# Ten 32-byte tiles made ahead of the weights' pool: 320 bytes further on for three pools

## The chip, the cores and the metric

The kernel runs on one core of one Trainium2 chip. The metric is device time of one execution in microseconds; the kernel before takes 1852.08 us (median of 3 runs, 1851.85 to 1852.86). The engines named below are PE (TensorE: matmuls, and beside them PEld, its weight loads), ACT (ScalarE), DVE (VectorE), POOL (GpSimd) and SP (SyncE, which here issues most DMAs). On-chip memory (SBUF) has 128 partitions; a tile lies at the same byte address in each of them, and "address" below is that byte address in a partition.

## What is computed

One layer on x of 256 rows by 2048 columns, in float32:

```python
x = x + 0.5 * swiglu(rms_norm(x, ffn1_norm), ffn1_w_gate, ffn1_w_up, ffn1_w_down)
proj = rms_norm(x, mix_norm) @ w_in                      # u | q | k | v, 1024 columns each
y_ssm = s5_mixer(u, ...)                                 # diagonal state space, gelu, GLU
y_sb = stick_breaking_attention(rms_norm(q), rms_norm(k), v)     # 8 heads of 128
x = x + concat(rms_norm(y_ssm), rms_norm(y_sb)) @ w_out
x = x + 0.5 * swiglu(rms_norm(x, ffn2_norm), ffn2_w_gate, ffn2_w_up, ffn2_w_down)
gate = sigmoid(rms_norm(x, ple_norm) @ w_ple_gate)
x = x + rms_norm((p @ w_ple_proj) * gate, ple_post_norm)
```

The two feed-forward blocks have an inner width of 5632; their six weight matrices are most of the work.

## The kernel before, in words

**Products in two parts.** Each float32 operand is split into a high part in the matmul's own format (fp32r) and a low part, the rest: `split` (line 178) casts on ACT at line 181 (`whi` from `raw`) and subtracts on DVE at line 184 (`wlo`). A product is then three matmuls: high by high (line 305), high by low (306), low by high (310). In every one of them the weights (`whi`, `wlo`; 512 columns) are the moving operand and the activations (`nhi`, `nlo`, `hhi`, `hlo`; 128 by 128) the stationary one, which a weight load brings in just before. Only the GLU of the state-space branch (lines 1369 to 1378) has it the other way round, with 256 moving columns.

**Where weights go.** SP loads 1 MB of weights at a time into one of five `raw` buffers; ACT and DVE make `whi` and `wlo` of it, two rows of 512 at a time, in four buffers each; `gemm_half` (line 298) runs 12 matmuls on each such pair for both halves of the rows of x, or 6 for one half.

**`Seven`.** In the feed-forward blocks, two neighbouring blocks of columns are worked together (class `Seven`, line 446). Its `column` (524) is `gemm_half` for one half of the rows at a time. Its `chunk` (490) takes two 1 MB loads and does with seven products of six matmuls (lines 480, 481, 483 in `product`) what would be eight: four of the seven have sums of weights as moving operand. DVE makes a sum (`sum`, line 487), ACT casts it into `shi`, DVE subtracts into `slo`. The stationary operand of a chunk is a plain activation or a sum of activations; both lie in the tiles of the activations.

**The last stage.** `w_ple_proj` is multiplied by `p`, split into two tiles `pT`. For the last block of columns `gemm_resident` (line 341) keeps half of the gate's weights and all of the projection's in tiles `whi`, `wlo` of the stage's own memory.

**Where tiles lie.** Pools take their memory one behind the other in the order in which they are made (lines 52 to 56). Memory of single stages (`phase`, line 73: sums of the feed-forward blocks, their `hT`, the state-space and attention tiles, the last stage) begins behind the last of them. A tile's size is rounded up to 32 bytes, and the program keeps 1152 bytes for itself at the start. So in the kernel before:

| pool | tiles | begins at | begins modulo 512 |
|---|---|---|---|
| const | six masks of 512 bytes, then 1416 (rounded to 1440) and 128 | 1152 | 128 |
| wts | 5 `raw` or `x` of 8192; 4 `whi` and 4 `wlo` of 4096 | 5792 | 160 |
| act | 4 `nhi`, 4 `nlo`, 2 `hhi`, 2 `hlo`, 4096 each | 79520 | 160 |
| com | `h` twice and `sg` of 4096, `sq` of 2048, `mid` of 8192 | 128672 | 160 |
| small | 10 `sm` of 32 | 151200 | 160 |
| stages | `shi`, `slo`, `sum`, `hT`, `pT`, `q`, `k`, ... | 151520 | 480 |

Tiles of wts, act, com and most of the stages are multiples of 512 bytes, and so are the steps inside them that the matmuls take (512, 1024 or 2048 bytes): every such operand begins where its pool begins, modulo 512.

**What sets the order.** The order of each engine's instructions follows the program text; small pieces of work are put between the matmuls by counted steps (`put_off`, `step`). Engines wait for each other by semaphores.

Of the kernel before, what the change touches and what calls it, by code (L numbers as in the profile page):

```python
# [33 lines left out]
def layer_kernel(ctx: ExitStack, tc: tile.TileContext, a: dict, shapes: dict, out: bass.AP):  # L34
# [15 lines left out]
    assert TT == 2 and NP == 64 and HC == 16 and DH == P and NC == 64 and SW == NH * DH  # L50

    cpool = ctx.enter_context(tc.tile_pool(name="const", bufs=1))
    wp = ctx.enter_context(tc.tile_pool(name="wts", bufs=4))
    actp = ctx.enter_context(tc.tile_pool(name="act", bufs=1))
    comp = ctx.enter_context(tc.tile_pool(name="com", bufs=1))
    smp = ctx.enter_context(tc.tile_pool(name="small", bufs=10))
    dramp = ctx.enter_context(tc.tile_pool(name="scratch", bufs=1, space=bass.MemoryType.DRAM))
    accp = ctx.enter_context(tc.tile_pool(name="acc", bufs=4, space=bass.MemoryType.PSUM))
    auxp = ctx.enter_context(tc.tile_pool(name="aux", bufs=2, space=bass.MemoryType.PSUM))
# [1602 lines left out]
```

## Time and profile before

| | |
|---|---|
| median of the runs | 1852.08 us (1851.85 to 1852.86) |
| the profiled execution's own time | 1852.7 us |
| its span, first to last instruction | 1850.6 us |
| PE busy | 1838.3 us, 99% of the span, 9032 matmuls |
| DVE busy | 1460.6 us, 79% |
| ACT busy | 1027.4 us, 56% |
| DMA | 406.36 MB, mean 220 GB/s |

The profile's page has the span in total and in slices, the chain of work that ended last, and groups of instructions by line and tile. [...] What a matmul costs when PE never stops is the step from its start to the start of the next one, which the timeline shows: start in us, length in us, engine, line, operation, tiles, count. A row with x2 or x4 holds that many matmuls in a row.

### The profile page before, as it was taken

What the parts mean: (1) busy time and instruction counts of PE and PEld (TensorE: products, weight loads), DVE (VectorE), ACT (ScalarE), POOL (GpSimd) and SP (SyncE); (2) the same over time, 40 slices, a digit from 0 to 9 for tenths busy, and PEclk for the clock granted to TensorE, in tenths of its full rate; (3) what the DMA queues carried; (4) which work ended last, traced back from release to release, by engine and by line L of the source; (5) the groups of instructions that cost most, each with busy time, mean ns of one, the idle gap of its engine ahead of it and who ended that gap; (6) DMA issues with size and microseconds to landing.
All of it is one profiled execution on the core that took longest, in us unless ns stands there. A gap on an engine that the chain in (4) does not pass through costs nothing.

```text
span 1850.6 us, 23946 instructions
## 1 busy us (share of the span) xinstructions
PE 1838.3 (99%) x9032; PEld 1518.5 (82%) x9032; DVE 1460.6 (79%) x1718; ACT 1027.4 (56%) x1187; POOL 63.3 (3%) x108
## 2 busy tenths in 40 slices
PE   9999999999999999999999999999999999999998
PEld 7888888778888888888897888888888888888887
DVE  8967665998888876687567798989898978887665
ACT  7444443655564656365685565655555555565654
POOL 0011000000000000010021000000000000000000
PEclk9999999999999999999999999999999999999999
DMA  9888868566756567675646776665656675666663
GB/s 334 281 274 277 252 217 246 173 228 200 241 196 213 192 217 248 190 262 166 216 142 218 224 262 216 235 206 198 218 198 219 207 244 185 223 195 217 208 219 125
DMA packets 232307, 406.36 MB, mean 220 GB/s; under 512 B 26784, under 2 KB 50720, under 8 KB 231904
## 3 DMA queue, kind: packets, MB, share of 16 engines
q1 hardware_dynamic: 227824, 392.81, 63.8%
q0 software_dynamic: 3648, 10.62, 1.8%
q8 instruction: 70, 1.15, 0.2%
q10 hardware_dynamic: 720, 1.41, 0.2%
q14 instruction: 45, 0.37, 0.1%
HBM read 373.46 MB, written 11.93 MB: 208 GB/s over the span
## 4 chain that ended last, share of the span: by engine, by line
PE 92%; DVE 3%; DMA 2%; ACT 2%; SPq 1%; issue 1%; DVEq 0%; ACTq 0%
PE acc L305 18%; PE acc L310 18%; PE acc L306 18%; PE aux L305 7%; PE aux L306 7%; PE aux L310 7%; PE acc L480 3%; PE acc L481 2%; PE acc L483 2%; PE aux L480 2%; PE aux L483 2%; PE aux L481 2%; DVE wlo L184 1%; SPq L1170 1%; DMA raw<-in_w_in 1%
## 5 line engine op out<-in xcount | busy, mean ns | idle before, releaser
L181 ACT CAST whi<-raw 128x1024 fp32r<-128x1024 f32 x639 | 668.1, 1052 | 684.8 <-PE acc L306 388.9
L184 DVE TENSOR_TENSOR wlo<-raw,whi 128x1024 fp32r<-128x1024 f32 x639 | 772.0, 1221 | 297.9 <-ACT whi L181 295.1
L305 PE MATMUL acc<-whi,nhi 128*128 128x512 f32 x1232 | 482.9, 392 | 1.8 <-ACT whi L181 1.7
L306 PE MATMUL acc<-whi,nlo 128*128 128x512 f32 x1232 | 479.9, 390 | 0.0
L310 PE MATMUL acc<-wlo,nhi 128*128 128x512 f32 x1232 | 340.6, 389 | 0.2 <-DVE wlo L184 0.2
L305 PEld LDWEIGHTS acc<-whi,nhi 128*128 128x128 f32 x1232 | 231.5, 188 | 52.2 <-ACT whi L181 3.0
L310 PEld LDWEIGHTS acc<-wlo,nhi 128*128 128x128 f32 x1232 | 231.2, 188 | 48.8 <-DVE wlo L184 0.6
L306 PEld LDWEIGHTS acc<-whi,nlo 128*128 128x128 f32 x1232 | 231.6, 188 | 47.2
L306 PE MATMUL acc<-whi,hlo 128*128 128x512 f32 x376 | 146.4, 389 | 0.0
L305 PE MATMUL acc<-whi,hhi 128*128 128x512 f32 x376 | 146.3, 389 | 0.0
L181 ACT CAST shi<-sum 128x1024 fp32r<-128x1024 f32 x108 | 113.4, 1052 | 43.1 <-DVE sum L487 39.6
L306 PE MATMUL aux<-whi,hlo 128*128 128x512 f32 x344 | 133.8, 389 | 0.0
L305 PE MATMUL aux<-whi,hhi 128*128 128x512 f32 x344 | 133.8, 389 | 0.0
L184 DVE TENSOR_TENSOR slo<-sum,shi 128x1024 fp32r<-128x1024 f32 x108 | 130.9, 1216 | 0.6 <-ACT shi L181 0.5
L310 PE MATMUL acc<-wlo,hhi 128*128 128x512 f32 x376 | 114.6, 389 | 0.2 <-DVE wlo L184 0.2
L310 PE MATMUL aux<-wlo,hhi 128*128 128x512 f32 x344 | 106.0, 389 | 0.0
L306 PE MATMUL aux<-whi,nlo 128*128 128x512 f32 x240 | 93.4, 389 | 0.0
L305 PE MATMUL aux<-whi,nhi 128*128 128x512 f32 x240 | 93.4, 389 | 0.0
L306 PEld LDWEIGHTS acc<-whi,hlo 128*128 128x128 f32 x376 | 70.6, 188 | 15.1 <-DVE hlo L184 0.4
L310 PEld LDWEIGHTS acc<-wlo,hhi 128*128 128x128 f32 x376 | 70.5, 188 | 15.2 <-DVE wlo L184 0.6
L305 PEld LDWEIGHTS acc<-whi,hhi 128*128 128x128 f32 x376 | 70.6, 188 | 14.6
L306 PEld LDWEIGHTS aux<-whi,hlo 128*128 128x128 f32 x344 | 64.6, 188 | 13.5
(345 smaller groups left out, 2162.6 us busy)
## 6 DMA issues: line engine op xcount, KB each, us to landing
raw<-in_ffn_w_up SPq DMA_DIRECT2D x88, 1024.0 KB, 5.8
raw<-in_ffn_w_down SPq DMA_DIRECT2D x88, 1024.0 KB, 5.1
raw<-in_ffn_w_gate SPq DMA_DIRECT2D x86, 1024.0 KB, 6.2
raw<-in_w_in SPq DMA_DIRECT2D x32, 1024.0 KB, 5.7
raw<-in_w_out SPq DMA_DIRECT2D x16, 1024.0 KB, 5.3
raw<-in_w_ple_gate SPq DMA_DIRECT2D x16, 1024.0 KB, 5.1
hT<-mid SPq DMA_DIRECT2D x160, 64.0 KB, 3.5
h<-mid SPq DMA_DIRECT2D x176, 32.0 KB, 3.6
```

What stands on the lines that cost most here:

```text
L181: copy = nc.scalar.copy(hi, src)
L184: nc.vector.tensor_tensor(out=lo, in0=src, in1=hi.bitcast(F32), op=ALU.subtract)
L305: nc.tensor.matmul(ps[t], lhsT=lh, rhs=hi[:, j, cols], start=start and j == 0, stop=False)
L306: nc.tensor.matmul(ps[t], lhsT=ll, rhs=hi[:, j, cols], start=False, stop=False)
L310: nc.tensor.matmul(ps[t], lhsT=lh, rhs=lo[:, j, cols], start=False, stop=stop and j == 1)
L480: nc.tensor.matmul(ps, lhsT=lh[j], rhs=hi[:, j], start=begin and j == 0, stop=False)
L481: nc.tensor.matmul(ps, lhsT=ll[j], rhs=hi[:, j], start=False, stop=False)
L483: nc.tensor.matmul(ps, lhsT=lh[j], rhs=lo[:, j], start=False, stop=z in final and j == 1)
L1170: nc.sync.dma_start(zt[0][p1 : p1 + HC, z], sv[p0 : p0 + HC, r % 2 * 2 + r // 2])
```

## The change

The pool `small` is made directly behind `const`, ahead of `wts`, instead of behind `com`. Its ten tiles of 32 bytes now lie at 5792, and wts, act and com begin 320 bytes further on, at 6112, 79840 and 128992, which is 480 modulo 512. The stages begin where they did, at 151520, also 480 modulo 512. `const` stays at 128. No instruction, size, buffer count or wait is written differently.

```diff
     cpool = ctx.enter_context(tc.tile_pool(name="const", bufs=1))
+    smp = ctx.enter_context(tc.tile_pool(name="small", bufs=10))
     wp = ctx.enter_context(tc.tile_pool(name="wts", bufs=4))
     actp = ctx.enter_context(tc.tile_pool(name="act", bufs=1))
     comp = ctx.enter_context(tc.tile_pool(name="com", bufs=1))
-    smp = ctx.enter_context(tc.tile_pool(name="small", bufs=10))
```

## The prediction

> **What bounds the kernel now.** First the page's totals and its chain of waits, then the list of who waited for whom.
>
> ```profile
> span 1850.6 us, 23946 instructions
> PE 1838.3 (99%) x9032; PEld 1518.5 (82%) x9032; DVE 1460.6 (79%) x1718; ACT 1027.4 (56%) x1187; POOL 63.3 (3%) x108
> PEclk9999999999999999999999999999999999999999
> PE 92%; DVE 3%; DMA 2%; ACT 2%; SPq 1%; issue 1%; DVEq 0%; ACTq 0%
> ```
> ```profile
> ACT whi L181 <- PE acc L306: 388.9, 272, 3.0
> ACT whi L181 <- DMA raw<-in_w_in: 13.0, 4, 8.5
> PEld acc L480 <- ACT shi L181: 3.5, 2, 2.1
> PEld aux L480 <- ACT shi L181: 1.9, 3, 1.3
> PEld aux L483 <- DVE slo L184: 0.6, 1, 0.6
> ```
>
> PE is busy in 99% of the span, with the granted clock in its top tenth in every slice, and is 92% of the chain. ACT waits 388.9 us for PE to free a `whi` buffer; PE waits for its makers in a handful of places only. So the time is the number of matmuls times their step, and I look for what sets the step. In the timeline of PE, four stretches without a wait, with operands that begin at different places (the table of pools gives the places):
>
> ```profile
> 1150.11 0.39 PE L305 MATMUL acc<-whi,nhi 128*128 128x512 f32 x1
> 1150.33 0.39 PE L306 MATMUL acc<-whi,nlo 128*128 128x512 f32 x1
> 1150.56 0.39 PE L305 MATMUL acc<-whi,nhi 128*128 128x512 f32 x1
> 1150.79 0.39 PE L306 MATMUL acc<-whi,nlo 128*128 128x512 f32 x1
> 1151.01 0.62 PE L310 MATMUL acc<-wlo,nhi 128*128 128x512 f32 x2
> 1151.47 0.39 PE L305 MATMUL acc<-whi,nhi 128*128 128x512 f32 x1
> ...
> 1163.71 0.39 PE L305 MATMUL aux<-whi,nhi 128*128 128x512 f32 x1
> ```
> ```profile
> 1785.90 0.40 PE L305 MATMUL acc<-whi,pT 128*128 128x512 f32 x1
> ...
> 1788.70 0.40 PE L305 MATMUL acc<-whi,pT 128*128 128x512 f32 x1
> ...
> 1791.50 0.39 PE L305 MATMUL acc<-whi,nhi 128*128 128x512 f32 x1
> ...
> 1813.29 0.40 PE L305 MATMUL acc<-whi,pT 128*128 128x512 f32 x1
> ...
> 1816.09 0.40 PE L305 MATMUL acc<-whi,nhi 128*128 128x512 f32 x1
> ...
> 1821.60 0.39 PE L305 MATMUL acc<-whi,nhi 128*128 128x512 f32 x1
> ```
>
> - Both operands at 160 modulo 512 (weights in wts, activations in act): ten groups of six from 1150.11 to 1163.71, 13.60 us / 60 = **226.7 ns** a matmul.
> - Moving at 160, stationary at 480 (`pT`, from 1785.90): two blocks of 12 in 5.60 us, **233.3 ns**. The block from 1813.29 to 1816.09 says the same: 2.80 / 12.
> - Moving at 480, stationary at 160 (the resident `whi` and `wlo` of the last stage, 24 of them from 1816.09 to 1821.60): 5.51 / 24 = **229.6 ns**.
>
> Width, type and clock are the same in all three; what differs is where the operands begin. Unlike operands cost 2.9 to 6.6 ns a matmul. What both at 480 would cost, which is what the change makes, is seen only with 256 columns, in the last stage; beside it the GLU, both at 160:
>
> ```profile
> 923.82 0.28 PE L1369 MATMUL acc<-hhi,whi 128*128 128x256 f32 x1
> ...
> 925.50 1.12 PE L1378 MATMUL acc<-hhi,wlo 128*128 128x256 f32 x8
> ```
> ```profile
> 1840.10 0.28 PE L305 MATMUL acc<-whi,pT 128*128 128x256 f32 x1
> ...
> 1840.58 0.40 PE L310 MATMUL acc<-wlo,pT 128*128 128x256 f32 x2
> 1840.82 1.02 PE L1554 MATMUL aux<-x,ident 128*128 128x512 f32 x2
> ```
>
> Both at 160: 14 matmuls in 1.68 us, 120.0 ns. Both at 480: 6 in 0.72 us, 120.0 ns. So what counts in these rows is whether the two begin alike, not where.
>
> **The change, part by part.** It adds and removes no instruction, DMA, buffer or wait, and moves none past another on a queue; it moves wts, act and com by 320 bytes, and the ten small tiles ahead of them.
>
> *Products with operands in wts and act.* These are nearly all; they are alike before (160) and after (480). I take 0 for them, by the two equal rows of 120.0 ns; the other bound stands in the last rival.
>
> *Chunks of `Seven`.* The sums lie in the stages (480), their partners in act (160): unlike now, alike after. One chunk without a wait, from its first product with a sum:
>
> ```profile
> 1091.27 0.40 PE L480 MATMUL acc<-shi,nhi 128*128 128x512 f32 x1
> ...
> 1096.78 0.40 PE L480 MATMUL acc<-whi,hhi 128*128 128x512 f32 x1
> ...
> 1099.55 0.39 PE L305 MATMUL acc<-whi,nhi 128*128 128x512 f32 x1
> ```
> ```profile
> L181 ACT CAST whi<-raw 128x1024 fp32r<-128x1024 f32 x639 | 668.1, 1052 | 684.8 <-PE acc L306 388.9 <-PE aux L306 146.0 <-PE acc L481 61.3
> L181 ACT CAST shi<-sum 128x1024 fp32r<-128x1024 f32 x108 | 113.4, 1052 | 43.1 <-DVE sum L487 39.6 <-PE acc L481 2.7 <-issue 0.3
> L181 ACT CAST hhi<-hT 128x1024 fp32r<-128x1024 f32 x56 | 58.4, 1043 | 0.9 <-PE aux L310 0.8
> ```
>
> The four products with sums (24 matmuls) take 5.51 us, 229.6 ns each, like the resident weights. The two behind them have both operands at 160 and still take 2.77 us / 12 = 231 ns: a disturbed sequence needs a dozen matmuls to fall back to 226.7. Together 36 in 8.28 us, where 36 x 226.7 = 8.16: **0.12 us a chunk**. There are 108 casts of sums, four a chunk, so 27 chunks: 3.24 us. Rounding of the rows (0.01 us) leaves 3.0 to 3.5.
>
> *The last stage.* `pT` in three blocks, 36 x 6.6 ns = 0.24 us; resident weights against activations, 24 for each half of the rows, 48 x 2.9 ns = 0.14 us; the falling back behind them, by half a chunk's tail, 0.07 us. Together 0.45 us.
>
> *The casts and subtractions.* `whi` from `raw` (both at 160) and `shi` from `sum` (both at 480) take 1052 ns alike; `hhi` from `hT`, unlike today, 1043. When it becomes alike I allow 9 ns more for 56 of them, 0.5 us of ACT, hidden: ACT is at 56% and waits for PE. If that cover were gone it would be 0.5 us.
>
> *DMAs into moved tiles.*
>
> ```profile
> raw<-in_ffn_w_up SPq DMA_DIRECT2D x88, 1024.0 KB, 5.8
> hT<-mid SPq DMA_DIRECT2D x32, 32.0 KB, 3.9
> h<-mid SPq DMA_DIRECT2D x176, 32.0 KB, 3.6
> ```
>
> Between tiles that begin unlike (`mid` to `hT`) 32 KB land in 3.9 us, between like ones (`mid` to `h`) in 3.6. The change would make the former like the latter; 0.3 us nobody waits for, since `hT` is read in the later half of a feed-forward block. The weights' DMAs keep their sizes; that 320 bytes change a 5.8 us transfer shows in no row, so from both sides I use that same 0.3 us. ACT's four waits for `w_in` (13.0 us) are the place where it would be felt: 4 x 0.3 = 1.2 us either way; I take 0.
>
> *The masks* stay at 128 and were unlike their partners before (160 or 480); they stay unlike. 0.
>
> Sum: 3.24 + 0.45 = **3.7 us less**. The profiled execution's own time is 1852.7 us (2.1 us more than its span) and would become 1849.0; it lies 0.6 us above the median, so the median becomes 1852.1 - 3.7 = **1848.4 us**.
>
> [...]
>
> **The rivals.** The measurement of this kernel can tell about 0.2% from no change, 3.7 us: a faster result is one below 1848.4, which is just where the sum ends.
>
> *The gain is kept whole* (0.56): 3.4 to 4.2 us with the rounding and 0.2 us from settling behind other short waits. 1847.9 to 1848.7.
>
> *Part of it becomes waiting* (0.26). In a chunk the sums come just in time from DVE and ACT. The rows of PEld show six such waits. There, an earlier PE waits longer: up to 0.12 us each, 0.7 us in all; as much again if chunks that now just don't wait begin to. 1848.7 to 1849.9. Against it: with six waits, at least 21 of 27 chunks have none.
>
> *Nothing changes* (0.10). The extra steps would belong to sums and to `pT` for another reason than where they lie, such as many stationary tiles in turn, or all would be swallowed at the waits. 1852.1, between 1851.4 and 1852.7. For it: even like operands within a chunk take 231 ns. Against it: resident `whi` differ from the others only in their place.
>
> *Beginning at 480 costs by itself, for each operand* (0.08): 2.9 ns for the moving one, 6.6 for the stationary one. Then the change puts 9.5 ns on what is now at 226.7.
>
> ```profile
> L305 PE MATMUL acc<-whi,nhi 128*128 128x512 f32 x1232 | 482.9, 392 | 1.8 <-ACT whi L181 1.7
> L305 PE MATMUL acc<-whi,hhi 128*128 128x512 f32 x376 | 146.3, 389 | 0.0
> L305 PE MATMUL aux<-whi,hhi 128*128 128x512 f32 x344 | 133.8, 389 | 0.0
> L305 PE MATMUL aux<-whi,nhi 128*128 128x512 f32 x240 | 93.4, 389 | 0.0
> ```
>
> These four are 2192 matmuls, and lines 306 and 310 have as many: 6576 x 9.5 ns = 62 us, 1914 us. It decides from little: 0.6 ns each is 3.7 us, and with the 3.7 us gained, 1.1 ns makes the kernel slower by 0.2%. Against it stand the two rows of 120.0 ns, which a sum of two prices can't give, but they are six matmuls of half the width.
>
> **How the numbers follow.** The forecast is the likeliest case, 1848.4 us. Its own range straddles the line of 0.2%: of its 0.56 I put 0.48 beyond it (what isn't in the sum, the settling behind other waits and DMAs between tiles that become alike, can only add) and 0.08 short of it. With 0.26 and 0.10 of the next two that makes faster 0.48, same 0.44, slower 0.08. The range for 8 in 10 takes in the first two cases, 1847.9 to 1849.9, and the 1.2 us of DMAs on both sides: 1846.7 to 1851.1; it leaves out 0.18.
>
> **What the profile after would show.** Right: steps of 226.7 ns through a whole chunk (36 matmuls in 8.16 us), for `pT` and for resident weights, and still 226.7 ns for `whi` against `nhi`. Matmul lengths near 389 ns in the groups of `shi` and `pT`. Wrong: unlike steps as before with all operands alike; or a step other than 226.7 ns in the plain groups, which would move the time by 6.6 us for every nanosecond; or longer waits for `shi` and `slo` that take up what the steps give.

## The result and the profile after

The changed kernel takes 1849.42 us (median of 22 runs, 1848.27 to 1850.12), the kernel before in the same comparison 1851.97 us (22 runs, 1851.4 to 1852.86). The ratio is 0.9986, 95% interval 0.998 to 0.9992: 2.55 us less, between 1.5 and 3.7. Two later comparisons of the same two kernels gave 3.63 and 3.52 us less (below). The profiled execution took 1849.88 us with a span of 1847.8; the one of before 1852.7 with 1850.6, so the profiles to be compared are 2.8 us apart.

The page of the changed kernel, its totals and the head of its chain of waits:

```profile
span 1847.8 us, 23946 instructions
PE 1835.1 (99%) x9032; PEld 1518.8 (82%) x9032; DVE 1460.7 (79%) x1718; ACT 1027.3 (56%) x1187; POOL 65.1 (4%) x108
PE 92%; DVE 3%; ACT 1%; DMA 1%; SPq 1%; issue 1%; DVEq 0%; ACTq 0%
```

The instructions and their order on each engine are the same as before. PE is busy 3.2 us less (1838.3 before), ACT and DVE are unchanged within 0.1 us, PE is still 92% of the chain. So the time went out of PE's matmuls, and PE's timeline shows where. The same chunk as in the prediction (start in us, length, engine, line, operation, tiles, count):

```profile
1090.18 0.39 PE L480 MATMUL acc<-shi,nhi 128*128 128x512 f32 x1
...
1095.62 0.39 PE L480 MATMUL acc<-whi,hhi 128*128 128x512 f32 x1
...
1098.34 0.39 PE L305 MATMUL acc<-whi,nhi 128*128 128x512 f32 x1
```

The four products with sums take 5.44 us (5.51 before), the two behind them 2.72 us (2.77): 36 matmuls in 8.16 us, 226.7 ns each, and no falling back is left. Then a plain stretch of `gemm_half`, and the last stage:

```profile
1148.66 0.39 PE L305 MATMUL acc<-whi,nhi 128*128 128x512 f32 x1
...
1160.90 0.39 PE L305 MATMUL aux<-whi,nhi 128*128 128x512 f32 x1
```
```profile
1783.52 0.39 PE L305 MATMUL acc<-whi,pT 128*128 128x512 f32 x1
...
1788.95 0.39 PE L305 MATMUL acc<-whi,nhi 128*128 128x512 f32 x1
...
1813.43 0.39 PE L305 MATMUL acc<-whi,nhi 128*128 128x512 f32 x1
...
1818.88 0.39 PE L305 MATMUL acc<-whi,nhi 128*128 128x512 f32 x1
```

The plain stretch, both operands now at 480 instead of 160, has 54 matmuls in 12.24 us, 226.7 ns as before. `pT` has 24 in 5.43 us, 226.3 ns (233.3 before), and the resident weights have 24 in 5.45 us, 227.1 ns (229.6). From the first of these four rows to the last are 35.36 us, where before there were 35.70.

The prediction says that both operands at 480 are seen before the change with 256 columns only. That overlooks six matmuls of 512 columns in the profile before, resident weights against `pT`:

```profile
1827.05 0.39 PE L305 MATMUL acc<-whi,pT 128*128 128x512 f32 x1
...
1828.43 0.39 PE L305 MATMUL acc<-whi,nhi 128*128 128x512 f32 x1
```

They took 1.38 us, 230 ns each, although both operands begin at 480. In the changed kernel the same six take 1.36 us, 226.5 ns. What went before them is the difference: a stretch with both operands at 160 in the kernel before, at 480 in the changed one. The first experiment shows the same steps where both operands move on together.

The groups by line and tile say it for many at once (matmuls in the group, busy us, mean ns of one). First those of the changed kernel, then the same of before:

```profile
L480 PE MATMUL aux<-shi,nhi 128*128 128x512 f32 x84 | 32.9, 392 | 0.0
L480 PE MATMUL acc<-shi,hhi 128*128 128x512 f32 x54 | 21.0, 389 | 0.0
L305 PE MATMUL acc<-whi,pT 128*128 128x512 f32 x14 | 5.4, 389 | 0.0
L305 PE MATMUL acc<-whi,nhi 128*128 128x512 f32 x1232 | 483.0, 392 | 2.1 <-ACT whi L181 1.6 <-ACT whi L273 0.3
```
```profile
L480 PE MATMUL aux<-shi,nhi 128*128 128x512 f32 x84 | 33.2, 396 | 0.0
L480 PE MATMUL acc<-shi,hhi 128*128 128x512 f32 x54 | 21.3, 394 | 0.0
L305 PE MATMUL acc<-whi,pT 128*128 128x512 f32 x14 | 5.6, 397 | 0.0
```

A matmul is 4 to 8 ns shorter where a partner was moved to begin alike, and the big group of `whi` and `nhi`, which moved as a whole, stays at 392.

Over all float32r matmuls of 512 columns, I summed what each step between starts exceeds 226.5 ns by, with the steps in which PE waits left out: 6.17 us before, 2.61 after. So about 3.6 us of steps went, and the spans differ by 2.8: some 0.8 us came back as waiting in these two executions.

### The profile page after: what moved, and what is told of

It reads as the page before. It is cut to its first block, busy times and chain, and to the rows that moved or that the text cites. A ratio compares the mean times of both kernels' runs of the same rounds, so it can differ in the third digit from the quotient of the medians.

```text
span 1847.8 us, 23946 instructions
## 1 busy us (share of the span) xinstructions
PE 1835.1 (99%) x9032; PEld 1518.8 (82%) x9032; DVE 1460.7 (79%) x1718; ACT 1027.3 (56%) x1187; POOL 65.1 (4%) x108
## 4 chain that ended last, share of the span: by engine, by line
PE 92%; DVE 3%; ACT 1%; DMA 1%; SPq 1%; issue 1%; DVEq 0%; ACTq 0%
PE acc L305 18%; PE acc L310 18%; PE acc L306 18%; PE aux L305 7%; PE aux L306 7%; PE aux L310 7%; PE acc L480 2%; PE acc L481 2%; PE acc L483 2%; PE aux L483 2%; PE aux L480 2%; PE aux L481 2%; SPq L1170 1%; DVE wlo L184 1%; DMA raw<-in_w_in 1%
## 5 line engine op out<-in xcount | busy, mean ns | idle before, releaser
L181 ACT CAST shi<-sum 128x1024 fp32r<-128x1024 f32 x108 | 113.5, 1052 | 43.1 <-DVE sum L487 39.4
L305 PEld LDWEIGHTS aux<-whi,hhi 128*128 128x128 f32 x344 | 64.6, 188 | 13.4
```

Of the source, the lines that this page charges most:

```text
L181: copy = nc.scalar.copy(hi, src)
L305: nc.tensor.matmul(ps[t], lhsT=lh, rhs=hi[:, j, cols], start=start and j == 0, stop=False)
```

## Where 0.8 us of the gain went

Some waits of PEld in the changed kernel (in total, times, longest one, us), and behind them one group of the kernel before:

```profile
PEld acc L480 <- ACT shi L181: 3.6, 2, 2.1
PEld aux L480 <- ACT shi L181: 2.1, 3, 1.4
PEld acc L310 <- DVE wlo L184: 1.6, 3, 0.6
PEld acc L305 <- ACT whi L273: 1.4, 3, 0.7
PEld aux L483 <- DVE slo L184: 0.5, 1, 0.5
```
```profile
PEld acc L305 <- ACT whi L273: 0.9, 3, 0.5
```

The five waits for `shi` were 3.5 and 1.9 us before, now 3.6 and 2.1: 0.3 us longer together. The three largest, near 337, 365 and 407 us, are 1.3, 1.4 and 2.1 us before and come out the same in every profiled execution of the changed kernel (1.4, 1.5 and 2.1 us). DVE and ACT, which make the sums, are busy as long as before (1460.7 and 1027.3 us); at 337 and 365 us PE waits 0.1 us longer for them, out of the 0.12 us that a chunk gains. That is how a chunk's gain is lost in the few chunks that had such a wait before.

The waits for `whi` of line 273 grew more, by 0.5 us. They all lie in the first 11 us, ahead of any chunk, and are 1.4 and 1.0 us in two later executions of the changed kernel. What sets them no run shows.

The wait for `slo` stands at another place than before. The one of 0.6 us at 633 us is gone in all three profiled executions of the changed kernel. One at 515 us is new, in a chunk that had none, and it is in all three, with 0.5, 0.2 and 0.2 us. These are rows of the whole timeline there, first of the changed kernel, then of a later execution of the same program (the idle time before an instruction is in brackets):

```profile
514.21 1.22 DVE L184 TENSOR_TENSOR slo<-sum,shi 128x1024 fp32r<-128x1024 f32 x1
...
515.48 0.30 PEld L483 LDWEIGHTS aux<-slo,nhi 128*128 128x128 f32 x2 [0.51 <-DVE slo L184]
```
```profile
513.88 1.22 DVE L184 TENSOR_TENSOR slo<-sum,shi 128x1024 fp32r<-128x1024 f32 x1
...
515.15 0.30 PEld L483 LDWEIGHTS aux<-slo,nhi 128*128 128x128 f32 x2 [0.22 <-DVE slo L184]
```

The waits of DVE in that window name what was late:

```profile
DVE sum L487 <- DMA raw<-in_ffn_w_down: 0.5, 1, 0.5
```
```profile
DVE sum L487 <- DMA raw<-in_ffn_w_down: 0.2, 1, 0.2
```

DVE waited 0.3 us longer for this load in the one execution than in the other, and PE 0.3 us longer for `slo`. The 0.6 us of `wlo` at 1664 us in the first profile is not there at all in the later one, whose span is 1846.6 us, 4.0 below that of before. So part of what came back belongs to the program (the longer waits for `shi`, some 0.2 us at 515 us), and part comes and goes.

## The experiments

**PE alone, operands at chosen places.** The layer is left out: 35 sequences of 48 matmuls of 512 columns, each with moving and stationary operand at places of its own. `at` returns a slice of a tile that begins at the wanted place modulo 512.

```diff
-    ... (the whole layer)
+    for c, (name, rm, rs) in enumerate(CASES):
+        acc = ps.tile([P, 512], F32, tag="acc", name=f"{name}_0")
+        for i in range(N):
+            tc.keep_in_program_order(nc.tensor.matmul(
+                acc, lhsT=at(st, ST, rs, i % 8, P, 256), rhs=at(mv, MV, rm, i // 2 % 4, 512, 512),
...
```

> PE alone: 35 sequences of 48 matmuls of 512 columns, the moving and the stationary operand beginning at chosen places modulo 512; no other engine works beside it, and the layer isn't computed. Relative places count (my theory): 226.7 ns a step wherever both begin alike (eight such sequences at 0, 64, ... 448), 233.3 ns where the stationary one lies 320 bytes further on, 229.6 ns where it lies 192 bytes further on, and something in between for the others. Places themselves count: the alike sequences differ among each other by up to 9.5 ns. Other engines' work beside PE counts: 226.7 ns in all 35.

Rows of PE's timeline, one per sequence (start, from the first start to the last end, name, count). `sg`, `si` and `sk` have the stationary operand 192, 256 and 320 bytes further on than the moving one; `ba` to `bd` have both alike, at 0, 64, 128 and 192:

```profile
80.11 11.16 PE L43 MATMUL sg<-mv,st 128*128 128x512 f32 x48
91.11 11.36 PE L43 MATMUL sh<-mv,st 128*128 128x512 f32 x48
102.31 11.05 PE L43 MATMUL si<-mv,st 128*128 128x512 f32 x48
113.19 11.35 PE L43 MATMUL sj<-mv,st 128*128 128x512 f32 x48
124.38 11.36 PE L43 MATMUL sk<-mv,st 128*128 128x512 f32 x48
135.59 11.40 PE L43 MATMUL sl<-mv,st 128*128 128x512 f32 x48
...
268.99 11.08 PE L43 MATMUL ba<-mv,st 128*128 128x512 f32 x48
279.91 11.08 PE L43 MATMUL bb<-mv,st 128*128 128x512 f32 x48
290.83 11.08 PE L43 MATMUL bc<-mv,st 128*128 128x512 f32 x48
301.75 11.08 PE L43 MATMUL bd<-mv,st 128*128 128x512 f32 x48
```

From one start to the next: `sg` 11.00 us / 48 = 229.2 ns, `si` 10.88 / 48 = 226.7, `sk` 11.21 / 48 = 233.5. With the first dozen steps of each sequence left out, as the passage from the one ahead, the single steps give:

| stationary minus moving, bytes | step, ns |
|---|---|
| 0 (eight places, 0 to 448) | 226.7 |
| 4, 8, 16, 48 | 232.4, 230.7, 233.4, 233.4 |
| 32, 64, 160, 224 | 233.3 to 233.4 |
| 96 | 234.3 |
| 128 | 232.4 |
| 192 | 228.8 |
| 256 | 226.7 |
| 288 to 480 | as 256 less (from start to start 320 gives 233.5 and 64 233.3; 448 and 192 both 229.2) |

The same distances with the moving operand shifted instead agree within 0.1 ns (256 gives 226.7, 192 gives 228.9, 64 gives 233.3). With next to nothing else running (DVE is busy in 2% of this span, ACT in 2%, at its start), PE's settled step goes in these sequences with the distance of its two operands, not with either place (226.7 ns at all eight alike), and a distance longer by 256 gives the same step: 226.7 ns at 0 and 256, 11.00 us for the 48 at 192 and at 448. One distance, 128, has two values in two runs (see the end). The three steps of the kernel before are in the table: `pT` at 320 from its moving operand is 64 in the table (233.4; 233.3 in the kernel), sums and resident weights with the activation at -320 are 192 (228.8; 229.6 in stretches of 24 that include the passage).

A change of place has a price of its own. `bb` and `bc` each follow a sequence that is just as alike, 64 bytes lower, and take 10.92 us from start to start, 227.5 ns, where `si` takes 226.7. The first ten steps of `bb` are 229, 229, 233, 236, 224, 231, 236, 228, 233 and 231 ns, the others 226.7. The six matmuls of `pT` at 1827.05 us in the kernel before have the steps 228, 229, 234, 236, 224 and 231: after such a change, of both operands at once, `bb` needs ten matmuls until 226.7 ns are reached.

**The small tiles between wts and act.** Weights stay at 160; act, com and the stages begin at 480. Now nearly all products are unlike, and the sums are alike.

```diff
     wp = ctx.enter_context(tc.tile_pool(name="wts", bufs=4))
+    smp = ctx.enter_context(tc.tile_pool(name="small", bufs=10))
     actp = ctx.enter_context(tc.tile_pool(name="act", bufs=1))
     comp = ctx.enter_context(tc.tile_pool(name="com", bufs=1))
-    smp = ctx.enter_context(tc.tile_pool(name="small", bufs=10))
```

> The small tiles between weights and activations: weights begin at 160, activations, com and stages at 480 modulo 512, so that nearly all products are unlike by 320 bytes. Relative places count: 233.3 ns a step in 7062 matmuls of 512 columns in place of 226.7, 46.6 us more, less the 3.4 us that the chunks and resident weights lose by becoming alike: 1895 us. The stages' memory is what costs: 1849 to 1852 us, as only the stages have the slow steps. Other engines' work in the chunks is what costs: 1849 to 1852 us too.

1892.76 us (one run; before, on the same chip, 1852.5), 40.3 us more. A plain stretch in PE's timeline, and the big group:

```profile
1180.17 0.39 PE L305 MATMUL acc<-whi,nhi 128*128 128x512 f32 x1
...
1192.77 0.39 PE L305 MATMUL aux<-whi,nhi 128*128 128x512 f32 x1
```
```profile
L305 PE MATMUL acc<-whi,nhi 128*128 128x512 f32 x1232 | 490.0, 398 | 1.4 <-ACT whi L181 1.4
```

54 matmuls in 12.60 us are 233.3 ns each; the group's mean goes from 392 to 398 ns. The trace has some 6950 matmuls of weights from wts against activations between which PE doesn't wait: at 233.3 for the 227.0 they averaged before, 43.8 us. The 688 with sums or resident weights come down from 229.8 to 227.8 ns, 1.4 us, and the waits between matmuls of 512 columns shrink from 14.2 to 12.0 us; that a PE with longer steps comes later to its operands is my reading of it, which no row shows by itself. That leaves 40.2 us, where the spans differ by 40.0. My 1895 us had left out the waits and counted every matmul at 226.7 before.

**The activations first.** Pools in the order act, small, wts, com: activations at 160, weights, com and stages at 480.

```diff
-    wp = ctx.enter_context(tc.tile_pool(name="wts", bufs=4))
     actp = ctx.enter_context(tc.tile_pool(name="act", bufs=1))
-    comp = ctx.enter_context(tc.tile_pool(name="com", bufs=1))
     smp = ctx.enter_context(tc.tile_pool(name="small", bufs=10))
+    wp = ctx.enter_context(tc.tile_pool(name="wts", bufs=4))
+    comp = ctx.enter_context(tc.tile_pool(name="com", bufs=1))
```

> Activations first, then the small tiles, then weights and com: activations begin at 160, weights, com and stages at 480 modulo 512, the other way round than with the small tiles in between. Relative places count: 229.6 ns a step in 7062 matmuls, 20.5 us more than the kernel before; the chunks' sums stay at 229.6 and p becomes alike (0.2 us less): 1872 us. The stages' memory or other engines' work is what costs: 1849 to 1852 us.

1863.44 us (one run; before 1852.5), 10.9 us more. The same two views:

```profile
1160.47 0.39 PE L305 MATMUL acc<-whi,nhi 128*128 128x512 f32 x1
...
1172.84 0.39 PE L305 MATMUL aux<-whi,nhi 128*128 128x512 f32 x1
```
```profile
L305 PE MATMUL acc<-whi,nhi 128*128 128x512 f32 x1232 | 484.9, 394 | 2.3 <-ACT whi L181 1.5 <-ACT whi L273 0.8
```

54 in 12.37 us are 229.1 ns, so the kind of unlikeness matters: the same two places with the roles exchanged cost 2.4 ns a matmul instead of 6.6. My expectation of 1872 us was too high by 8.6. About half of that is the step: 229.6 ns comes from stretches of 24 that include the passage from one distance to the other, and the settled step is 229.0. A quarter is the average before, 227.0 ns and not 226.7. Some 6950 matmuls x 2.0 ns = 13.9 us, less 0.8 for sums and `pT` and 1.1 of waits between matmuls of 512 columns, gives 12.0. Another 1.2 us are gone from the steps of narrower matmuls, which I can't put down to places or to waits. That leaves 10.8; measured 10.9.

**The changed kernel again, twice.** No edit.

> The changed kernel once more, for a second profile of the same program. If the 3.7 us of steps were partly taken back by waits that belong to the program, the same waits of PE stand at the same places as in the first profile (1.3 us at 336 us, 1.4 us at 365 us, 2.0 us at 407 us, 0.25 us at 515 us, 0.5 us at 1664 us). If they are the landing of DMAs in this or that execution, those at 515 and 1664 us are gone or elsewhere. The time is 1848.7 to 1850.2 us in either case.

> The changed kernel a third time, against the kernel before, in five rounds, for the size of the gain. The steps' gain of 3.6 us is the same in every execution, and what differs are waits for DMAs that land late in one or the other: 0.9981 to 0.9985 of the time before. If the gain of 2.5 us of the first comparison is the whole of it: 0.9986.

| comparison | before | after | ratio, 95% interval |
|---|---|---|---|
| first | 1851.97 (22 runs) | 1849.42 (22) | 0.9986, 0.998 to 0.9992 |
| second | 1852.5 (13) | 1848.87 (10) | 0.9982, 0.9972 to 0.9992 |
| third | 1852.74 (15) | 1849.22 (11) | 0.9982, 0.9973 to 0.9991 |

The differences of the medians lie between 2.5 and 3.6 us. The intervals overlap widely, so the three don't contradict each other, and none of them tells 2.55 from 3.6. The steps' part is nearly the same in every profile: the sum of what exceeds 226.5 ns is about 2.5 and 2.3 us in the two later ones, 3.7 and 3.9 less than before. Of the two waits that I had named as tests, the one at 1664 us is gone in both, the one at 515 us is in both, shorter (0.2 us): neither expectation holds for all of them.

**PE alone, in steps of 4 bytes.** Whether some distance is better than alike: 64 sequences with the stationary operand 0 to 252 bytes further on than a moving one at 160, and eight with the moving one at 480. The layer is left out.

```diff
-CASES = [(f"s{chr(97 + k)}", 160, (160 + 32 * k) % 512) for k in range(16)]
+CASES = [("n" + "abcdefgh"[k // 8] + "abcdefgh"[k % 8], 160, 160 + 4 * k) for k in range(64)]
+CASES += [("q" + "abcdefgh"[k], 480, (480 + d) % 512) for k, d in enumerate((-4, -16, 4, 16, 192, 248, 256, 264))]
```

> PE alone again, 72 sequences of 48 matmuls; the stationary operand lies 0, 4, 8, ... 252 bytes (modulo 512) further on than the moving one, and then, with the moving one at 480, by -4, -16, 4, 16, 192, 248, 256 and 264 bytes. The layer isn't computed. What the first map showed holds with a period of 256 bytes (my theory): 226.7 ns at 0 and at 256, 228.9 at 192, 232.4 at 4 and 230.7 at 8, the same at 260-like places (264 as 8), and no place is below 226.7 ns, so that alike is the best there is. Rival: some place between the multiples of 32 is below 226.7 ns; every nanosecond less would be worth 6.6 us in the whole kernel, and a version with that distance would beat both.

Groups of PE (48 matmuls each; busy us, mean ns), at distances of 164, 192, 256, 228 and -4:

```profile
L41 PE MATMUL nfb<-mv,st 128*128 128x512 f32 x48 | 11.5, 400 | 0.0
...
L41 PE MATMUL nga<-mv,st 128*128 128x512 f32 x48 | 11.2, 392 | 0.0
...
L41 PE MATMUL qg<-mv,st 128*128 128x512 f32 x48 | 11.1, 389 | 0.0
...
L41 PE MATMUL nhb<-mv,st 128*128 128x512 f32 x48 | 11.0, 389 | 0.0
L41 PE MATMUL qa<-mv,st 128*128 128x512 f32 x48 | 11.0, 389 | 0.0
```

The first sequence, at distance 0, runs into the start-up and says nothing; 0 is taken from the experiment above. Elsewhere no settled step is below 226.7 ns. 237.3 at 164 is the highest. Six distances beside 0 and 256 also give 226.7: 120, 132, 144, 156, 228 and 252 (which is -4). So alike is as good as any of the distances tried, all multiples of 4 bytes, and there is nothing further to gain from them at this width; no other version of the kernel was run.

## Why the prediction came out as it did

*What bounds the kernel, and what sets the step*: right. PE alone shows the same three steps at the same distances (226.7, 228.8 and 233.4 ns, in the kernel 226.7, 229.6 and 233.3), so neither ACT, DVE nor a DMA has a part in them.

*Products in wts and act at 0*: right. Their stretch stays at 226.7 ns, and the eight places alike in the experiment agree. The ground for it was thinner than it looked: the two equal rows of 120.0 ns are six matmuls of half the width, and the six of full width with both at 480, which the prediction overlooked, took 230 ns.

*Chunks, 0.12 us each and 3.24 us in all; last stage 0.45 us; sum 3.7*: right to 0.2 us, as 3.6 us of steps are gone (3.7 and 3.9 in the two later profiles). The chunk shown went from 8.28 to 8.16 us. The stretch of the last stage that is shown gives 0.34 us; the second 24 resident products, 0.07 us by the same 2.9 ns, lie behind it.

*Casts and DMAs*: the two allowances did not show. `hhi` from `hT` was to take 1052 ns once alike, and `hT` from `mid` was to land in 3.6 us (before: 1043 ns and 3.9 us). The changed kernel has:

```profile
L181 ACT CAST hhi<-hT 128x1024 fp32r<-128x1024 f32 x56 | 58.5, 1045 | 1.8 <-PE aux L310 1.7
```
```profile
hT<-mid SPq DMA_DIRECT2D x32, 32.0 KB, 4.1
h<-mid SPq DMA_DIRECT2D x176, 32.0 KB, 3.7
```

So the difference between these rows belongs to the tiles or the moment, not to where they begin. Nothing on the path hung on it.

*The forecast of 1848.4 us*: the median is 1849.42, 1.0 us above, within the range. It is 0.14% below the kernel before, and 0.18% in the later comparisons: short of the line of 0.2%, so of the three outcomes "same" came (0.44) and not the slightly likelier "faster" (0.48). Of the first comparison's missing microsecond the profiles account for 0.8: waits, among them 0.3 us more for `shi` and 0.5 us more at the start of the kernel. The step that was too firm is "at least 21 of 27 chunks have none" as the ground for keeping all: one of those chunks has a wait now, at 515 us. The rival *Part of it becomes waiting* (1848.7 to 1849.9) holds all three medians by their times. By their differences, the second and third (3.6 and 3.5 us) are in the 3.4 to 4.2 us of *The gain is kept whole*. So both cases are in the data and the runs do not part them.

*Nothing changes*: refuted by the steps above, and by the 40.3 and 10.9 us that the order of the pools alone cost. *Beginning at 480 costs by itself*: refuted by the eight equal places, 226.7 ns each. That would have been 62 us.

## What to carry to other kernels

Where PE is the bound (here 92% of the chain), look at the start-to-start step of its matmuls in stretches without a wait and compare them between operands from different pools; here they were 226.7, 229.6 and 233.3 ns for equal shapes at a granted clock of 1.000, and the operands' places made the difference. Then try an order or a padding of the pools with which moving and stationary operands begin alike, the largest group first: in this kernel one order of the pools costs 40 us and another gains 3, and with PE alone, at 512 columns, alike modulo 256 bytes gave 226.7 ns at every place tried. Look also for a gain that comes back as waiting where operands are made just in time: here some 0.8 of 3.6 us in the first profile.

## What the runs showed that I had not expected

- The steps repeat after 256 bytes: 226.7 ns at a distance of 256 in both runs with PE alone, as at 0, where I had written everything modulo 512. Nor do all other distances lie between 226.7 and 233.3 ns: 96 gives 234.3, 164 gives 237.3.
- The two directions differ: 64 costs 6.7 ns, 192 (which is -64) costs 2.1, against 226.7 alike.
- Steps at an unlike distance are not evenly longer but repeat a pattern of a few matmuls: 226, 229, 232 ns at 192; 231 and 236 at 64; 228, 230, 233, 241, 232, 231, 232 at 128. No run looks inside: why the distance counts at all, and why 120, 132, 144, 156, 228 and 252 also give 226.7 ns, stays open. All of it holds for 512 columns of float32r with 128 by 128 stationary; other shapes were not run.
- At 128 the two runs with PE alone differ, 232.4 and 233.5 ns, at the same two places (160 and 288) and with another pattern, where all other shared distances agree within 0.1. So the distance alone doesn't settle the step there; what else does is open.
